# A hybrid encoder layer: the DVE steps of the triangular solve are given 36 units of other work in place of 24

## The chip, the core and the metric

The kernel runs on one core of one Trainium2 chip. The metric is the device time of one execution in microseconds; the time shown for a kernel is the median of its runs. The core has five engines with instruction queues of their own: TensorE (PE, with its weight loads shown apart as PEld), VectorE (DVE), ScalarE (ACT), GpSimd (POOL) and SyncE (SP, which issues most DMAs). Each works its queue off in order. An instruction that waits for another engine stops everything behind it in its own queue.

## The reference, cut to what matters

One layer over 2048 prompt rows and 8 x 16 sample rows of width 1024. Of the projected columns, 768 go to sliding-window attention and 1824 to an RWKV-7 mixer with 8 heads of 64; then come an output projection and a squared-ReLU feed-forward of width 4096:

```python
h = _rms(x, ln1_g)
p = h @ w_in
...
def step(S, inp):
    r_t, w_t, k_t, v_t, a_t, b_t = inp
    sa = jnp.einsum('bhij,bhj->bhi', S, a_t)
    S = S * w_t[:, :, None, :] + sa[..., None] * b_t[:, :, None, :] + v_t[..., None] * k_t[:, :, None, :]
    y = jnp.einsum('bhij,bhj->bhi', S, r_t)
    return S, y
...
x = x + jnp.concatenate([att, rw], axis=-1) @ w_out
u = jax.nn.relu(_rms(x, ln2_g) @ w_up)
x = x + (u * u) @ w_down
```

The kernel doesn't walk through the recurrence token by token. It takes chunks of 64 tokens, and within a chunk the coupling of the tokens is a unit lower triangular system of 64 x 64 per head. Its inverse is the "solve" of this document.

## The kernel before, in words

**Tiles and stages.** The rows are 17 tiles of 128: 0 to 15 are the prompt, 16 (`SMP`) the samples. The input projection (`in_proj`, matmuls at line 210) takes tiles 0 to 3 and 16, then 4 to 7, 8 to 11 and 12 to 15, in nine column pieces each. The feed-forward takes five groups of tiles: three tiles each in groups 0 to 3, and 12 to 16 in group 4. For each of 32 slices of the hidden width, `up` (line 1230) multiplies and squares; after every two of them `down` (line 1252) adds into `y`, by a DVE instruction for each bank (line 1254). All weights are used as a high and a low part. They are split at first use, by ACT (line 128) and POOL (line 132), and written back to DRAM for the next groups.

**Streams.** Attention, the mixer's preparation (`prep_stream`) and its chain over chunks (`chain_stream`) are Python generators. For each tile, in the order 0, 1, 2, 16, 3, 4, ... 15, `prep_stream` loads the projected rows, forms decays and keys, transposes them on PE (line 594), multiplies the coupling matrices (line 613) and calls `solve`; then the chain takes the tile. A generator yields a pair (units of other work wanted before it goes on, its own matrix work).

**The solve (line 648 on).** On DVE: four transposes bring the diagonal 16 x 16 blocks of `ma` into `WS` (line 653); six pairs of multiply (line 666) and reduce (line 668) invert the 8 x 8 blocks; lines 674 and 677 do that for the 16 x 16 blocks; lines 685, 686 and 689 write the inverses into `so` twice (once for the sample tile), for both orders of indices. Then, for prompt tiles only, PE takes over with four products of 16 matmuls of 64 x 64 (`product`, line 704), with a DVE or ACT step on all 128 columns after each (lines 709, 713, 717, 721), which fill the blocks off the diagonal. The first product reads `so` as the last line-689 transposes left it.

**What sets the order.** `Weaver` writes the instructions of the streams between those of the main work (`filler`: the projection or the feed-forward). Its clock is not time but units of matrix work: the filler and the streams add their own. A stream that yielded u units is due u times its pace later. The pace of prep and chain is 0.75, and 0.88 in the feed-forward. In the projection every due stream goes on after each piece of filler work. In the feed-forward there are slots:

```python
                if self.clock < self.slot:
                    continue
                for m in list(self.mains):
                    while self.step([m], 2.0):
                        pass
                self.slot = self.clock + 3.2
```

In a slot each stream goes on as long as it is due within 2.0 units. A group of the feed-forward waits until its tiles are in `done`. The last group's buffers take the place of the mixer's: once all tiles are done during group 3, its set-up (`stages`: loads, mixes, output projection at line 1188, norms with transposes at line 1143) is spread evenly over what is left of group 3's 32 steps. The other groups are set up in one block between two groups.

The launch uses a framework with a scheduler of its own (`schedule_with_timeline_sim=True`): the order written is a priority, and an instruction may be placed ahead of others that were written before it. The order that runs is the one after that.

Of the kernel before, what the change touches and what calls it, by code (L numbers as in the profile page):

```python
# [34 lines left out]
def hymba_kernel(  # L35
# [454 lines left out]
    def rw_prep(t, rp, loaded, so):  # L490
# [117 lines left out]
        for par in range(2):  # L608
# [12 lines left out]
            yield 4, 1  # L621
        pr = dict(t=t, art=art, m1=m1, lam=lam, ma=ma, so=so)
        yield from solve(ma, pr["so"], not smp, rp)

        yield "tail"
# [23 lines left out]
    def solve(ma, so, full, rp):  # L649
        EX, WS = rwc["EX"], rwc["WS"]  # L650
        for q in range(4):
            B, o = q // 2, 16 - 16 * (q % 2)
            ve.transpose(out=WS[32 * q:32 * q + 32, o:o + 512],  # L653
                         in_=ma[32 * B:32 * B + 32, :, 16 * q:16 * q + 16].rearrange("p s i -> p i s").unsqueeze(2)
                         .broadcast_to([32, 16, 2, 16]))
        Wv = WS[:, 16:528].rearrange("p (i j) -> p i j", i=16)
        blk = WS[:, 16:544].rearrange("p (b x) -> p b x", b=2)
        Db = blk[:, :, 0:256].rearrange("p b (i j) -> p b i j", i=8)
        ve.memset(blk[:, :, 0:256:33], 1.0)
        WT = rp.tile([P, 512], F32, name="tm", bufs=2)  # L660
        yield 4, 0
        for i in range(2, 8):
            if i in (5, 7):
                yield 4, 0
            tmp = WT[:, 0:2 * i * i].rearrange("p (b x y) -> p b x y", b=2, x=i)
            ve.tensor_tensor(out=tmp, in0=Db[:, :, i, 0:i].unsqueeze(2).broadcast_to([P, 2, i, i]),  # L666
                             in1=Db[:, :, 0:i, 0:i].rearrange("p b j a -> p b a j"), op=ALU.mult)
            ve.tensor_reduce(out=Db[:, :, i, 0:i], in_=tmp, axis=AX.X, op=ALU.add)

        tmp = WT[:, 0:512].rearrange("p (i a j) -> p i a j", i=8, a=8)  # L670
        zz = rp.tile([P, 64], F32, name="zz").rearrange("p (i a) -> p i a", i=8)
        L21 = Wv[:, 8:16, 0:8]
        for lh, rh, dst in ((L21, Db[:, 0, :, 0:8], zz), (Db[:, 1, :, 0:8], zz, L21)):
            ve.tensor_tensor(out=tmp, in0=lh.unsqueeze(2).broadcast_to([P, 8, 8, 8]),
                             in1=rh.rearrange("p j a -> p a j").unsqueeze(1).broadcast_to([P, 8, 8, 8]), op=ALU.mult)
            yield 2, 0
            ve.tensor_reduce(out=dst, in_=tmp, axis=AX.X, op=ALU.add)
        gp.memset(so[64:96, :, 32:64], 0.0)
        Ev = EX[:, 16:272].rearrange("p (i j) -> p i j", i=8)[:, :, 0:16]
        for w in range(2):  # L680
            if w == 1 and not full:
                break
            yield 2, 0
            src = Wv[:, :, 0:16] if w == 0 else Wv[:, :, 0:16].rearrange("p i j -> p j i")
            ve.tensor_scalar(out=Ev, in0=src[:, 0:8], scalar1=lanes[0], scalar2=None, op0=ALU.mult)
            ve.scalar_tensor_tensor(out=Ev, in0=src[:, 8:16], scalar=lanes[1], in1=Ev, op0=ALU.mult, op1=ALU.add)
            for q in range(4):
                r0, o = 32 * (q // 2) + 64 - 64 * w, 16 - 16 * (q % 2)
                ve.transpose(out=so[r0:r0 + 32, :, 16 * q:16 * q + 16].rearrange("p s (b i) -> p i b s", b=2),  # L689
                             in_=EX[32 * q:32 * q + 32, o:o + 256])  # L690
        if not full:
            return
        yield 4, 0
        lo, hi = slice(0, 64), slice(64, 128)
        G = rp.tile([P, 1024], F32, name="t4").rearrange("p (a h x) -> p a h x", a=2, h=8)
        Z = [rp.tile([P, 512], F32, name="tm", bufs=2).rearrange("p (h x) -> p h x", h=8) for _ in range(2)]
        sc = [so[:, 8 * c:8 * c + 8] for c in range(2)]

        def product(terms):

            ps = psR.tile([P, 8, 64], F32, name="sv")
            for h in range(8):
                for c, (lh, rh) in enumerate(terms):
                    pe.matmul(ps[64 * c:64 * c + 64, h], lh[:, h], rh[:, h], start=True, stop=True)  # L704
            return [ps[lo], ps[hi]]

        p = product([(ma[lo, 8 * c:8 * c + 8], sc[c][lo]) for c in range(2)])
        for c in range(2):
            ve.tensor_tensor(out=G[hi, c], in0=p[c], in1=offm.unsqueeze(1).broadcast_to([64, 8, 64]), op=ALU.mult)
        yield 4, 1  # L710
        p = product([(G[hi, c], sc[c][hi]) for c in range(2)])
        for c in range(2):
            ve.tensor_tensor(out=sc[c][hi], in0=p[c], in1=sc[c][hi], op=ALU.add)
        yield 4, 1
        p = product([(G[hi, c], sc[c][hi]) for c in range(2)])
        for c in range(2):
            ac.copy(out=Z[c][hi], in_=p[c])
        yield 4, 1
        p = product([(G[hi, c], Z[c][hi]) for c in range(2)])
        for c in range(2):  # L720
            ve.tensor_tensor(out=sc[c][hi], in0=p[c], in1=sc[c][hi], op=ALU.add)
        yield 3, 1
# [719 lines left out]
```

## Time and profile before

| | |
|---|---|
| time, median of 3 runs | 3015.76 us (3009.49 to 3020.29) |
| the profiled execution's own time | 3006.76 us |
| its span in the profile | 3005.0 us |
| granted PE clock, mean of the span | 0.976 of full speed |
| PE busy | 2860.8 us, 95% |
| DVE busy | 1816.4 us, 60% |
| ACT busy | 866.6 us, 29% |
| POOL busy | 663.4 us, 22% |

The span is the time from the first to the last instruction of one profiled execution. Busy times count an engine's instructions with their overlap taken out; matmuls are pipelined, so a busy PE need not be at its peak. In the trace the input projection ends at about 925 us, group 0 runs from about 960 to 1360 us, group 1 from 1420 to 1790, group 2 from 1830 to 2165, group 3 from 2224 to 2555 and group 4 from there to the end; the stretches between are set-up. A matmul in 32-bit words on 64 columns appears twice in the trace where the program has it once, so a product's 16 matmuls are 32 there.

### The profile page before, as it was taken

Reading aid. Unit: us, or ns where it says so; the run is one execution under the profiler, and the core shown is the slowest. Engines: PE = TensorE matmul, PEld = TensorE weight load, DVE = VectorE, ACT = ScalarE, POOL = GpSimd, SP = SyncE. Lnnn points to the kernel's source line nnn. Section 1 sums busy time; section 2 is a strip of 40 time slices with the busy share of each in tenths; the row PEclk is TensorE's granted clock in tenths of the full one; section 3 lists DMA queues with packets and bytes.
Section 4 is the critical chain, followed back from the end, with each engine's and each line's share of the span. In section 5 each row is a group of like instructions: output and inputs, shape, how many; then the busy total and the mean of one; then the engine's idle time right before and its main releaser. Section 6 shows DMA issues by size and latency. Waiting matters only on the chain.

```text
span 3005.0 us, 52176 instructions
## 1 busy us (share of the span) xinstructions
PE 2860.8 (95%) x20746; PEld 2540.4 (85%) x20746; DVE 1816.4 (60%) x3411; ACT 866.6 (29%) x2093; POOL 663.4 (22%) x625
## 2 busy tenths in 40 slices
PE   7989999989997988989999999999999999999999
PEld 7978878878877877878888888888889999989988
DVE  3557687673775688786677875786633344344344
ACT  5342443443343433432222223222221021111111
POOL 2122432432434766751101110111000000000000
PEclk9999999999998999999999999999999999999999
DMA  7866565554748777877666675665676566544444
GB/s 267 292 217 196 174 209 180 181 175 155 235 157 298 284 269 286 293 265 252 217 228 235 231 270 179 240 215 201 223 293 242 210 218 239 180 154 149 147 154 147
DMA packets 192141, 657.71 MB, mean 219 GB/s; under 512 B 31885, under 2 KB 88989, under 8 KB 145818
## 3 DMA queue, kind: packets, MB, share of 16 engines
q1 hardware_dynamic: 176346, 557.64, 54.9%
q0 software_dynamic: 15552, 96.74, 7.8%
q8 instruction: 164, 2.69, 0.4%
q14 instruction: 79, 0.65, 0.1%
HBM read 486.37 MB, written 154.73 MB: 213 GB/s over the span
## 4 chain that ended last, share of the span: by engine, by line
PE 70%; DVE 14%; DMA 8%; issue 3%; ACT 2%; POOL 2%; SPq 0%; DVEq 0%; ACTq 0%; POOLq 0%
PE ffn L1230 21%; PE ffn L1252 21%; PE acc L210 11%; PE ffn L1188 3%; DMA w<-wp 2%; PE sv L704 2%; PE op L1188 2%; DVE so L689 2%; DMA xs<-pa 1%; DVE WS L653 1%; DMA pc<-pb 1%; DVE y L1254 1%; POOL w L132 1%; PE rk L613 1%; DVE tm L666 1%
## 5 line engine op out<-in xcount | busy, mean ns | idle before, releaser
L1230 PE MATMUL ffn<-ghh,w 128*128 128x384 f32 (+1 forms) x3072 | 779.2, 331 | 0.1
L1252 PE MATMUL ffn<-w,sh 128*128 128x512 f32 x2176 | 694.7, 401 | 17.3 <-DVE y L1254 13.9
L1230 PEld LDWEIGHTS ffn<-ghh,w 128*128 128x128 f32 x3072 | 548.8, 190 | 8.3 <-issue 2.9
L1254 DVE SCALAR_TENSOR_TENSOR y<-ffn,rs,y 128x512 f32<-128x512 f32 x544 | 401.8, 748 | 203.3 <-PE ffn L1252 201.6
L1230 PE MATMUL ffn<-ghl,w 128*128 128x384 f32 (+1 forms) x1536 | 505.9, 329 | 0.0
L1252 PEld LDWEIGHTS ffn<-w,sh 128*128 128x128 f32 x2176 | 403.8, 190 | 109.0 <-DVE y L1254 16.3
L210 PE MATMUL acc<-w,hh 128*128 128x304 f32 (+1 forms) x2128 | 463.9, 309 | 22.2 <-ACT ev L215 9.2
L1252 PE MATMUL ffn<-w,sl 128*128 128x512 f32 x1088 | 427.6, 396 | 2.4 <-DVE sl L1237 2.2
L210 PEld LDWEIGHTS acc<-w,hh 128*128 128x128 f32 x2128 | 351.0, 194 | 44.0 <-DMA w<-wp 11.2
L1235 DVE TENSOR_TENSOR tq<-tq 128x384 f32<-128x384 f32 (+1 forms) x192 | 111.4, 580 | 391.9 <-ACT tq L1234 391.0
L210 PE MATMUL acc<-w,hl 128*128 128x304 f32 (+1 forms) x1064 | 319.7, 303 | 0.0
L1234 ACT ACTIVATE tq<-ffn 128x384 f32<-128x384 f32 (+1 forms) x192 | 91.0, 474 | 709.4 <-PE ffn L1230 689.7
L1230 PEld LDWEIGHTS ffn<-ghl,w 128*128 128x128 f32 x1536 | 290.9, 189 | 5.2 <-issue 1.9
L1252 PEld LDWEIGHTS ffn<-w,sl 128*128 128x128 f32 x1088 | 205.7, 189 | 50.5 <-DVE sl L1237 4.7
L132 POOL TENSOR_TENSOR w<-ws,w 128x512 fp32r<-128x512 f32 x144 | 196.1, 1380 | 109.7 <-ACT w L128 104.7
L210 PEld LDWEIGHTS acc<-w,hl 128*128 128x128 f32 x1064 | 206.3, 194 | 3.9 <-issue 3.4
L1236 ACT CAST sh<-tq 128x384 fp32r<-128x384 f32 (+1 forms) x192 | 95.2, 496 | 344.6 <-PE ffn L1252 220.4
L1188 PE MATMUL ffn<-w,ghh 128*128 128x256 f32 x768 | 146.2, 291 | 19.5 <-ACT w L128 10.3
L1237 DVE TENSOR_TENSOR sl<-tq,sh 128x384 fp32r<-128x384 f32 (+1 forms) x192 | 117.1, 610 | 62.4 <-ACT sh L1236 62.2
L1188 PEld LDWEIGHTS ffn<-w,ghh 128*128 128x128 f32 x768 | 122.8, 196 | 22.6 <-ACT w L128 10.5
L215 ACT ACTIVATE ev<-acc,xr_rs 128x304 f32<-128x304 f32 (+1 forms) x153 | 75.9, 501 | 151.1 <-PE acc L210 103.9
L1188 PE MATMUL ffn<-w,ghl 128*128 128x256 f32 x384 | 110.2, 288 | 0.0
(349 smaller groups left out, 4084.8 us busy)
## 6 DMA issues: line engine op xcount, KB each, us to landing
w<-wp SPq DMA_DIRECT2D x288, 1024.0 KB
wp<-w POOLq DMA_DIRECT2D x72, 1024.0 KB, 7.3
w<-wp SPq DMA_DIRECT2D x72, 608.0 KB
w<-wp SPq DMA_DIRECT2D x36, 512.0 KB
ws<-in_wup_dram SPq DMA_DIRECT2D x32, 512.0 KB
ws<-in_wdn_dram SPq DMA_DIRECT2D x32, 512.0 KB
pb<-eb SPq DMA_DIRECT2D x102, 152.0 KB
pa<-ev SPq DMA_DIRECT2D x102, 152.0 KB
```

The source lines that it names most:

```text
L132: gp.tensor_tensor(out=wl[:, c], in0=ws[:, c], in1=wh[:, c].bitcast(F32), op=ALU.subtract)
L210: pe.matmul(acc[:, 0:n], a[:, kk], b[:, c], start=(kk == 0 and m == 0), stop=(kk == 7 and m == 2))
L215: ac.activation(out=ev, in_=acc[:, 0:n], func=AF.Copy, scale=hT[t][2])
L689: ve.transpose(out=so[r0:r0 + 32, :, 16 * q:16 * q + 16].rearrange("p s (b i) -> p i b s", b=2), in_=EX[32 * q:32 * q + 32, o:o + 256])
L1188: pe.matmul(pss[j // 2][:, o:o + 256], a[:, kk, self.col(t)], w[:, c], start=(kk == 0 and m == 0 and j % 2 == 0), stop=(kk == 7 and m == 2 ...
L1230: pe.matmul(ps, w[:, wc], a[:, kk, c], start=(kk == 0 and m == 0), stop=(kk == 7 and m == 2))
L1234: ac.activation(out=tq, in_=ps, func=AF.Relu)
L1235: ve.tensor_tensor(out=tq, in0=tq, in1=tq, op=ALU.mult)
L1236: ac.copy(out=sh[:, c], in_=tq)
L1237: ve.tensor_tensor(out=sl[:, c], in0=tq, in1=sh[:, c].bitcast(F32), op=ALU.subtract)
L1252: pe.matmul(ps, a[:, tc_], w[:, fc], start=(f == 0 and m == 0), stop=(f == 1 and m == 2))
L1254: ve.scalar_tensor_tensor(out=yt[:, c], in0=ps, scalar=self.rs2[t], in1=yt[:, c], op0=ALU.mult, op1=ALU.add)
```

## The change

Five yields in `solve` are made half as long again: 4 to 6, and 2 to 3. Three of these lines are met twice (in the loops), so a prompt tile's solve yields 36 units in place of 24: before the first row, before rows 5 and 7, between multiply and reduce of lines 674 and 677 (twice), before each of the two writings of `so`, and before the first product. No instruction is added or taken away.

```diff
         WT = rp.tile([P, 512], F32, name="tm", bufs=2)
-        yield 4, 0
+        yield 6, 0
         for i in range(2, 8):
             if i in (5, 7):
-                yield 4, 0
+                yield 6, 0
...
         for lh, rh, dst in ((L21, Db[:, 0, :, 0:8], zz), (Db[:, 1, :, 0:8], zz, L21)):
...
-            yield 2, 0
+            yield 3, 0
             ve.tensor_reduce(out=dst, in_=tmp, axis=AX.X, op=ALU.add)
...
         for w in range(2):
             if w == 1 and not full:
                 break
-            yield 2, 0
+            yield 3, 0
...
         if not full:
             return
-        yield 4, 0
+        yield 6, 0
         lo, hi = slice(0, 64), slice(64, 128)
```

**Tile 5's first product on PE, in group 0.** The names are the bank written, then the two operands; `w2` is a weight, `sh` and `sl` the high and low parts of the hidden values, `ma` the coupling matrices, `so0` the inverse. Before:

```order
L1252 MATMUL ffn_12452<-w2_12444,sl_12160 128x512
L1252 MATMUL ffn_12452<-w2_12444,sh_12294 128x512 x2
L1252 MATMUL ffn_12452<-w2_12444,sl_12295 128x512
L704 MATMUL sv_12425<-so0_2757,ma_12130 64x64 x16
L1252 MATMUL ffn_12460<-w2_12444,sh_12159 128x512 x2
L1252 MATMUL ffn_12460<-w2_12444,sl_12160 128x512
```

The change, at the same place of the `down` step, and where the last of the product stands:

```order
L1252 MATMUL ffn_12848<-w2_12840,sl_12592 128x512
L1252 MATMUL ffn_12848<-w2_12840,sh_12726 128x512 x2
L1252 MATMUL ffn_12848<-w2_12840,sl_12727 128x512
L704 MATMUL sv_13001<-so0_2757,ma_12562 64x64 x10
L1252 MATMUL ffn_12856<-w2_12840,sh_12591 128x512 x2
L1252 MATMUL ffn_12856<-w2_12840,sl_12592 128x512
```

```order
L1252 MATMUL ffn_12982<-w2_12966,sl_12883 128x512
L1252 MATMUL ffn_12990<-w2_12966,sh_12882 128x512 x2
L1252 MATMUL ffn_12990<-w2_12966,sl_12883 128x512
L704 MATMUL sv_13001<-so0_2757,ma_12562 64x64 x3
L1252 MATMUL ffn_13028<-w2_13020,sh_12770 128x512 x2
```

Of the 16 matmuls that stood together, ten stand at the same place of a `down` step, and the other six follow in pieces of one, two and three.

**The norms' transposes of group 4 on PE, within group 3** (`op` are the banks of its set-up, `y` its rows). Before, a piece of them between the matmuls of a `down` step:

```order
L1252 MATMUL ffn<-w_25361,sh 128x512 x2
L1252 MATMUL ffn<-w_25361,sl 128x512
L1143 MATMUL op<-cst,y 128x128 x6
L1252 MATMUL ffn<-w_25361,sh 128x512 x2
L1252 MATMUL ffn<-w_25361,sl 128x512
```

The change, in the last `up` step of group 3 and, between its matmuls, the first of group 4 (320 columns):

```order
L1230 MATMUL ffn<-ghh,w_26020 128x384
L1143 MATMUL op<-cst,y 128x128 x16
L1230 MATMUL ffn<-ghh,w_26179 128x320
L1230 MATMUL ffn<-ghl,w_26179 128x320
L1230 MATMUL ffn<-ghh,w_26179 128x320 x2
L1230 MATMUL ffn<-ghl,w_26179 128x320
L1230 MATMUL ffn<-ghh,w_26179 128x320 x2
L1143 MATMUL op<-cst,y 128x128 x8
```

Before, the 40 transposes stand in pieces of 1 to 7 over several steps; in the change they stand close together, in pieces of 4 to 16, where group 4 begins.

## Rows read from the trace of the kernel before

**Rows 1.** The page's first part: busy us (share of the span) x instructions of each engine.

```profile
PE 2860.8 (95%) x20746; PEld 2540.4 (85%) x20746; DVE 1816.4 (60%) x3411; ACT 866.6 (29%) x2093; POOL 663.4 (22%) x625
```

**Rows 2.** Windows by stage: length, busy us (x) of each engine, clock, DMA.

```profile
core 0: us, PE busy (x) PEld busy (x) DVE busy (x) ACT busy (x) POOL busy (x), PEclk, DMA share, GB/s
...
960.00:1360.00 400.00, 366.95 (x2659) 312.69 (x2660) 307.23 (x484) 158.07 (x293) 254.02 (x223) 0.95 0.79 281
...
1420.00:1790.00 370.00, 368.40 (x2764) 316.70 (x2761) 263.26 (x484) 94.56 (x214) 50.91 (x39) 0.99 0.65 227
...
1830.00:2165.00 335.00, 331.61 (x2448) 286.37 (x2448) 227.14 (x415) 78.56 (x175) 37.33 (x28) 0.99 0.61 212
2165.00:2224.00 59.00, 51.58 (x419) 48.20 (x420) 30.34 (x74) 18.62 (x47) 2.94 (x2) 1.00 0.88 340
2224.00:2555.00 331.00, 331.00 (x1894) 307.92 (x1895) 127.58 (x236) 54.45 (x122) 0.00 (x0) 1.00 0.64 226
```

**Rows 3.** Waits of PE and its weight loads: us in total, times, longest us.

```profile
PEld sv L704 <- DVE so L689: 19.8, 9, 7.1
...
PE sv L704 <- DVE so L689: 16.6, 6, 6.7
PE ffn L1252 <- DVE y L1254: 13.9, 10, 6.8
```

**Rows 4.** Timeline, PE: first products of tiles 1, 5, 7, 15 [idle before <-releaser].

```profile
404.64 1.12 PE L704 MATMUL sv<-so,ma 64*64 64x64 f32 x16 [3.22 <-DVE so L689]
...
1092.35 1.97 PE L704 MATMUL sv<-so,ma 64*64 64x64 f32 x32 [4.93 <-DVE so L689]
...
1311.19 1.97 PE L704 MATMUL sv<-so,ma 64*64 64x64 f32 x32 [6.70 <-DVE so L689]
...
2112.46 0.74 PE L704 MATMUL sv<-so,ma 64*64 64x64 f32 x18 [0.40 <-DVE so L689]
```

**Rows 5.** Timeline, DVE: tile 5's solve (start us, us, instruction).

```profile
1059.10 3.19 DVE L653 STREAM_TRANSPOSE WS<-ma 32x512 f32<-32x512 f32 x3
...
1078.33 2.25 DVE L674 TENSOR_TENSOR tm<-WS,zz 128x512 f32<-128x512 f32 x1
...
1082.77 0.35 DVE L686 SCALAR_TENSOR_TENSOR EX<-WS,cst,EX 128x128 f32<-128x128 f32 x1
...
1086.93 2.85 DVE L686 SCALAR_TENSOR_TENSOR EX<-WS,cst,EX 128x128 f32<-128x128 f32 x1
1089.82 2.47 DVE L689 STREAM_TRANSPOSE so<-EX 32x256 f32<-32x256 f32 x4
```

**Rows 6.** Timeline, DVE: the same two lines at tile 13.

```profile
1909.39 1.18 DVE L674 TENSOR_TENSOR tm<-WS,zz 128x512 f32<-128x512 f32 x1
...
1916.88 0.44 DVE L686 SCALAR_TENSOR_TENSOR EX<-WS,cst,EX 128x128 f32<-128x128 f32 x1
```

**Rows 7.** Timeline, POOL, beside tile 5's solve.

```profile
1083.75 2.49 POOL L132 TENSOR_TENSOR w<-ws,w 128x512 fp32r<-128x512 f32 x2 [1.14 <-ACT w L128]
...
1087.13 2.49 POOL L132 TENSOR_TENSOR w<-ws,w 128x512 fp32r<-128x512 f32 x2
```

**Rows 8.** The chain of waits: start us, us, engine and line, matmuls.

```profile
2237.98 8.20 PE ffn L1252 x36
2246.19 8.34 PE ffn L1230 x48
```

**Rows 9.** Windows of 5 us after the waits of tiles 5 and 7.

```profile
1090.00:1095.00 5.00, 2.65 (x34) 2.44 (x35) 4.93 (x8) 0.00 (x0) 0.48 (x1) 0.53 1.01 391
1095.00:1100.00 5.00, 5.00 (x21) 4.25 (x20) 3.40 (x6) 1.56 (x2) 0.19 (x1) 0.79 0.33 139
...
1310.00:1315.00 5.00, 3.81 (x37) 3.30 (x38) 4.93 (x8) 0.00 (x0) 0.00 (x0) 0.50 0.95 379
```

**Rows 10.** Timeline, PE: tile 4's second and third products.

```profile
964.45 1.15 PE L704 MATMUL sv<-so,t 64*64 64x64 f32 x32 [0.99 <-DVE t L709]
...
967.51 1.76 PE L704 MATMUL sv<-so,t 64*64 64x64 f32 x28 [1.33 <-DVE so L713]
```

## The prediction

> **What bounds the kernel now.** I read the page's busy times first [rows 1], then the stages by windows [rows 2], the waits [rows 3], and last the timelines around single solves [rows 4 to 7]. TensorE (PE) is busy for 95% of the span and DVE for 60% [rows 1], so PE sets the time, and a change in DVE's work pays only where PE stands still for it. Idle PE, as window length less busy time, is 33.0 us in the first feed-forward group (960 to 1360 us), but only 1.6 us in the next and 3.4 us in the one after [rows 2]. The time left to win by better cover is therefore in the input projection and in group 0, and not in the middle of the feed-forward.
>
> The change aims at one wait: PE's first solve product (line 704) on the last DVE step of the tile's solve (line 689). It costs PE 16.6 us in six waits, the longest 6.7 us. The weight loader's view of it is 19.8 us; the two overlap, so I do not add them [rows 3]. Three of the six carry most of it: tile 1 with 3.22 us in the input projection, tile 5 with 4.93 us and tile 7 with 6.70 us in group 0 [rows 4]. Later tiles pay 0.40 us, such as tile 15 [rows 4]. Why group 0 pays more stands in DVE's rows. At tile 5 the step at line 686 took 0.35 us once and 2.85 us the other time, and the product at line 674 took 2.25 us [rows 5], where at tile 13 the same lines took 0.44 and 1.18 us [rows 6]. While the slow ones ran, POOL was splitting weights (line 132), 2.49 us for each pair [rows 7], which it does only where weights are used for the first time.
>
> **What the change does.** It removes and adds no instruction. It only makes the Weaver wait longer between the solve's parts, and its arithmetic decides how much. In the feed-forward the pace is 0.88, slots are at least 3.2 units apart, and a stream goes on in the same slot if it is due within 2.0 units. A yield of 2 is due after 1.76 and went on at once; a yield of 3 is due after 2.64 and waits for the next slot. A yield of 4 or 6 (3.52 or 5.28) mostly takes one slot in either case. So the four small yields become four slots. Working the Weaver's clock through, a tile's period in the feed-forward grows from 92 units to 108, and the last tile's chain ends at 2049 in place of 1809. The feed-forward needs each group's tiles later than that in both, so it never waits for a tile.
>
> But what runs is the scheduler's order, not the Weaver's. For tile 5 DVE has 46 rows from the first line-653 transpose to the last line-689 one, ten of them the feed-forward's own, before and now alike: DVE's part is not spread out at all. On PE the first product is no longer in one piece. Its first 10 matmuls stand where all 16 stood, and the last five come about 14 us of matrix work later, as the order rows of the change show. I work such cover out from the matmuls in the order, at 8.34/48 = 0.174 us for one of 384 columns and 8.20/36 = 0.228 us for one of 512 [rows 8]. From the tile's last line-613 product to the head of the first solve product, PE has 23.7 us of work for tile 5 before and now; for tile 15, 22.3 us in both. A head of a few matmuls stops PE's queue as well as a whole product does, so its wait stays. The other products do move, by 15 to 20 us for most tiles, but nothing waited long for those.
>
> **The sum,** against the profiled execution (3006.76 us, of which 3005.0 us are span; the median of the runs shown, 3015.76 us, is 9.0 us above it, and I carry the difference over to that):
>
> 1. Tile 7's wait. With the longer period its solve moves from group 0's steady part to the stage between groups 0 and 1, where POOL no longer splits weights. I take its 6.70 us [rows 4] as gone. The granted clock was 0.50 in the 5 us that followed [rows 9], the lower of the two levels: 3.81 us of busy PE at half speed is 1.9 us more. Together -8.6 us. Bounds: -8.6 (gone) and 0 (its head now has 15.5 us of cover in place of 23.9, and waits there as long).
> 2. Tile 5's wait. Head and DVE rows are unchanged: 0. Bounds: 0 and, if all goes, -4.93 us and the slow clock behind it, (1 - 0.53) x 2.65 + (1 - 0.79) x 5.00 = 2.3 us [rows 4, 9]: -7.2 us.
> 3. Tile 3, now solved as the input projection ends. Its four products stand within 4 us of matrix work; before, they took 18 us. Each needs the DVE or ACT step on the one before it. The nearest rows are tile 4's, which waited 0.99 and 1.33 us between its products [rows 10]. Three such gaps at 1.2 us, less the 2.3 us that tile 4 no longer pays: about +1 us; without any cover three gaps of 2 us, +4. As the whole solve also has less cover (14.1 us before its head, where no tile had under 18.6), I take +3. Bounds 0 and +7.
> 4. Group 4's set-up. It is spread over group 3's 32 steps now, since tile 15 is done when that group begins. In the change it starts at step 26 and all 40 transposes of the normalised rows stand at the group's end, as the second pair of order rows shows. Before, group 3 had no idle PE at all in 331 us, while the set-up of group 3 itself, which stands in one block, lost 59.00 - 51.58 = 7.4 us [rows 2]. The new one lies between the two: +3 us. Bounds 0 and +7.4.
> 5. Everything else is moved and not changed. About half a tile's work leaves the input projection and group 0 for group 3, where DVE is busy for 127.6 of 331 us [rows 2]. It is still PE work there: 0. Bounds -5 and +5, three of the smaller waits [rows 3, 10] either way.
>
> Sum: -8.6 + 0 + 3 + 3 + 0 = about -3 us. On the median's scale 3013 us.
>
> One rule bears on term 2. The row shows the line-686 step at 2.85 us beside POOL's 2.49 us pair [rows 5, 7], and I keep its whole wait because the order beside it has not changed. The Trainium skill, SBUF — State Buffer, section "Who interferes with whom", says that a DVE instruction with two SBUF inputs and a GpSimd instruction that reads SBUF exclude each other for a whole instruction, and that issue order decides who blocks. By that rule the delay hangs on which of the two starts first, and so may be gone at tile 5 though its rows stand where they stood: the two stretched steps lost 2.85 - 0.44 and 2.25 - 1.18 us, 3.5 us in all [rows 5, 6], and the sum would be -6 us in place of -3.
>
> **The rivals.** A, *the wait goes after all* (faster). If the heads find their data ready, tiles 1, 5 and 7 lose 3.2, 7.2 and 8.6 us, and the 2.3 us at tile 4 go too: -21 us, 2995 us. For it: later products really have 15 us more in front of them, and POOL need not meet tile 5 again. Against it: the heads have not moved.
>
> B, *heads pulled forward into group 0* (slower). In the change tiles 4, 5 and 6 are solved there, and tile 4's first two matmuls stand behind 19.2 us of matrix work, while DVE needs 33.2 us for such a solve (1059.10 to the 1092.29 at which the last transpose ends) [rows 5]. Cover of 23.7 and 23.9 us meant a wait before, and tile 6 with 26.1 us had none, so it decides below about 24 us. If tile 4 then pays what tile 7 paid (8.6 us) and tile 7's own four early matmuls keep theirs, term 1 becomes +8.6, and with terms 3 and 4 the sum is +14.6 us: 3030 us. Against it: tile 4 had only 18.9 us before and no wait, because PE stood still for weights there.
>
> C, *it does not do what it says*: the heads keep every wait, tile 7's too, and the moves cancel: 3016 us, within my middle case.
>
> **How the numbers follow.** A difference of 0.3%, 9 us, is about what a measurement of this kernel can tell from none. The forecast with C around it, within 9 us of 3015.76, gets 0.50; A gets 0.29, since it needs only two of its three waits; B 0.21, since it needs a new wait at tile 4 or idle PE in both terms 3 and 4 at their upper ends. The range reaches from A's 2995 with 2 us below it to B's 3030: 2993 to 3030 us.
>
> **What would show it.** In the profile of the changed kernel: the wait of line 704 on line 689 should still be there, at about 16.6 - 6.7 = 10 us, tile 5's at 4 to 6 us and tile 7's under 1 us (term 1 is wrong if it is over 3). The waits between tile 3's products should sum to 3 to 6 us. Idle PE in the last 60 us of group 3 should be 1 to 6 us. Line 704 should run until late in group 3 in place of ending at its beginning, and the middle of the feed-forward (groups 1 and 2) should stay under 5 us of idle PE each. I am wrong if the line-704 wait falls under 5 us (then A, and the heads did not matter), if tile 4 waits over 4 us (then B), or if the input projection as a whole moves by more than 8 us, of which nothing here tells.

## The result and the profile after

The changed kernel takes **3062.89 us** (median; 3059.67 to 3066.61), the kernel before in the same runs 3013.75 us (3007.24 to 3020.29). The ratio is 1.0156, 95% interval 1.0141 to 1.0172: slower by 1.56%, 47 us. The prediction was 3013 us, range 2993 to 3030, with 0.21 on slower. It was wrong, in sign and in size.

The page's busy line of the change, which answers to [rows 1]:

```profile
PE 2885.9 (94%) x20746; PEld 2549.9 (83%) x20746; DVE 1809.9 (59%) x3411; ACT 862.7 (28%) x2093; POOL 659.0 (22%) x625
```

The span is 3064.8 us, 59.8 more than before. PE has the same 20746 matmuls, 25.1 us more busy time, and so 34.7 us more idle time. The two profiled executions lie further apart than the medians: 3006.76 us is near the lower end of the kernel before, and 3066.61 is the highest of the change's six. The granted clock differs too: 0.965 to 0.969 in the change's six executions (mean 0.968), 0.969 to 0.976 (mean 0.973) in 13 executions of the kernel before. If all of PE's busy time goes with it, that is 2885.9 x (1 - 0.968/0.973), about 15 of the 47 us; this is an estimate. To see where the idle time is, I cut both traces at the same events: the last projection matmul (line 210), the first `up` (line 1230) of group 0, the first output projection (line 1188) of group 1's set-up and of group 3's, and the first `up` of group 4. Before (windows; columns as in [rows 2]):

```profile
0.00:875.00 875.00, 807.70 (x6660) 723.54 (x6661) 549.89 (x1149) 348.02 (x981) 265.92 (x288) 0.97 0.62 205
875.00:970.00 95.00, 74.71 (x647) 65.85 (x646) 61.09 (x130) 38.23 (x86) 49.55 (x44) 0.84 0.71 255
970.00:1357.00 387.00, 356.27 (x2516) 303.28 (x2515) 295.80 (x454) 148.08 (x266) 246.76 (x216) 0.95 0.78 280
1357.00:2175.00 818.00, 803.88 (x6228) 696.94 (x6227) 578.06 (x1104) 206.74 (x479) 98.27 (x75) 0.99 0.64 225
2175.00:2544.00 369.00, 361.61 (x2171) 338.20 (x2170) 144.46 (x283) 67.05 (x154) 2.94 (x2) 1.00 0.68 243
```

The change, the same stages:

```profile
0.00:875.00 875.00, 799.36 (x6460) 717.18 (x6460) 535.44 (x1115) 339.75 (x962) 262.60 (x287) 0.96 0.62 205
875.00:998.00 123.00, 84.87 (x758) 73.91 (x753) 69.09 (x144) 44.53 (x103) 50.58 (x45) 0.78 0.57 201
998.00:1358.00 360.00, 337.66 (x2272) 288.80 (x2272) 260.07 (x384) 134.52 (x231) 230.90 (x206) 0.96 0.81 294
1358.00:2167.00 809.00, 781.25 (x5663) 676.33 (x5659) 527.11 (x1005) 186.60 (x430) 87.39 (x67) 0.98 0.64 226
2167.00:2599.00 432.00, 422.37 (x3062) 378.77 (x3061) 224.03 (x441) 91.68 (x212) 27.51 (x20) 0.98 0.61 217
```

These rows show work that was moved and not paid back. The set-up and steps of group 3 have 891 matmuls more (3062 against 2171) and are 63 us longer. The stages from which they came have 898 fewer: 200 in the projection, 244 in group 0, 565 in groups 1 and 2 with the set-ups before them, less 111 more in group 0's set-up. They should have become shorter by as much. But the projection, with 200 matmuls fewer, still takes 875 us, and the set-up of group 0 is 28 us longer; group 0 and the middle stage give back 27 and 9 us. The loss is made early, although the end shows it.

Length less busy time is PE's idle time. By stage, worked out from such windows, cut at the same events (the table's runs are explained below; a label's first part, such as e3, stands for the run):

| idle PE, us | projection | set-up 0 | group 0 | to group 3's set-up | group 3 with set-up | group 4 | sum | busy |
|---|---|---|---|---|---|---|---|---|
| before | 67.3 | 20.3 | 30.7 | 14.1 | 7.4 | 4.4 | 144.2 | 2860.8 |
| the change | 75.6 | 38.1 | 22.3 | 27.8 | 9.6 | 5.4 | 178.9 | 2885.9 |
| e3, projection only | 76.4 | 34.2 | 29.6 | 29.0 | 7.9 | 4.4 | 181.3 | 2873.3 |
| e4, feed-forward only | 66.5 | 19.1 | 20.0 | 19.1 | 11.1 | 4.3 | 140.1 | 2881.3 |
| e9, change without four tiles | 70.6 | 27.0 | 19.8 | 16.3 | 8.9 | 4.8 | 147.4 | 2880.4 |
| e5, tile 3 and all behind late | 66.6 | 20.7 | 34.1 | 27.1 | 9.5 | 4.3 | 162.4 | 2879.0 |
| s4, only those behind tile 3 late | 70.5 | 26.9 | 21.0 | 24.2 | 6.3 | 4.6 | 153.5 | 2862.8 |
| s3_pace | 74.5 | 21.5 | 34.6 | 13.5 | 6.4 | 4.4 | 154.7 | 2875.9 |
| e1, only the 4s longer | 79.5 | 17.8 | 29.6 | 26.1 | 6.2 | 4.4 | 163.6 | 2886.1 |
| e2, only the 2s longer | 79.5 | 20.1 | 11.9 | 22.3 | 8.2 | 4.7 | 146.7 | 2899.1 |
| p6_16, as fast as before | 64.9 | 18.7 | 35.0 | 23.2 | 4.3 | 4.3 | 150.5 | 2863.5 |

Each row is one execution. The last row tells how much a column moves without a loss: p6_16 is as fast as the kernel before, and its stage up to group 3's set-up has 23.2 us of idle PE against 14.1. So the 27.8 us of the change there are not shown to be a loss, but its 38.1 us in group 0's set-up stand well clear of the 18.7 to 26.9 of runs without a loss.

The waits of PE in the change, which answer to [rows 3] (us in total, times, longest):

```profile
PE sv L704 <- DVE so L689: 18.3, 8, 6.5
PE ffn L1143 <- DVE ghl L143: 16.6, 3, 8.1
PE ffn L1252 <- DVE y L1254: 14.2, 10, 6.9
PE ffn L1188 <- DVE y L1193: 13.7, 3, 9.9
PE acc L210 <- DMA w<-wp: 12.6, 13, 3.4
...
PE acc L210 <- DVE hl L86: 5.8, 4, 3.5
```

The wait that the change aims at is not smaller: 18.3 us against 16.6 [rows 3]. Four others grew. In the kernel before, the wait of line 1143 on line 143 was 6.2 us, that of line 1188 on line 1193 4.7, line 210 on its weights 8.5, and line 210 on line 86 2.1 us. The first and the third grow without a loss too (19.4 us for line 1143 in p6_16, 12.6 for the weights in s4_delay4); only the other two stand out. The largest single ones, on PE's timeline of the change:

```profile
647.23 0.55 PE L210 MATMUL acc<-w,hh 128*128 128x304 f32 x2 [3.53 <-DVE hl L86]
...
882.64 1.98 PE L704 MATMUL sv<-so,ma 64*64 64x64 f32 x32 [5.32 <-DVE so L689]
886.20 1.98 PE L704 MATMUL sv<-so,t 64*64 64x64 f32 x32 [1.58 <-DVE t L709]
...
970.97 0.80 PE L1188 MATMUL ffn<-w,ghh 128*128 128x256 f32 x2 [9.93 <-DVE y L1193]
...
997.28 1.11 PE L1143 MATMUL ffn<-cst,y 128*128 128x128 f32 x4 [8.14 <-DVE ghl L143]
...
1175.12 1.12 PE L704 MATMUL sv<-so,ma 64*64 64x64 f32 x16 [6.47 <-DVE so L689]
```

The first is in the projection, the next four in group 0's set-up. At 882.64 it is tile 3's solve, which now stands behind the last projection matmul (874.6 us); before, its first product ran at 836.1 us, with 40 us of projection left. The rows at 647.23, 970.97 and 997.28 are waits of the main work on DVE, which was held by the mixer's rows; the last row is tile 5's first product, in group 0. DVE, ahead of the waits at 647.23 and 970.97:

```profile
643.16 1.04 DVE L653 STREAM_TRANSPOSE WS<-ma 32x512 f32<-32x512 f32 x1
...
646.49 0.68 DVE L86 TENSOR_TENSOR hl<-acc,hh 128x512 fp32r<-128x512 f32 x1
...
965.50 0.63 DVE L498 TENSOR_TENSOR xs<-xs,pc 128x456 f32<-128x456 f32 x1 [6.70 <-DMA pc<-pb]
969.95 0.63 DVE L498 TENSOR_TENSOR xs<-xs,pc 128x456 f32<-128x456 f32 x1 [3.81 <-DMA pc<-pb]
970.50 0.75 DVE L1193 TENSOR_TENSOR y<-ffn,y 128x256 f32<-128x256 f32 x2
```

The sample tile's solve starts at 639.96 us (before, at 611.61), and the row at 643.16 is the last of its four transposes; the split of the next tile's normalised rows (line 86), for which the projection waits, comes behind them. At 965 DVE stands for the DMA of tile 4's rows (line 498), and behind that instruction, in DVE's queue, wait the additions of group 0's output projection (line 1193). Ahead of 997.28 DVE had tile 4's solve between the line-143 rows.

### The profile page after: what moved, and what is told of

Same layout as the page of the kernel before. It is cut to its first block, busy times and chain, and to the rows that moved or that the text cites. A ratio compares the mean times of both kernels' runs of the same rounds, so it can differ in the third digit from the quotient of the medians.

```text
span 3064.8 us, 52188 instructions
## 1 busy us (share of the span) xinstructions
PE 2885.9 (94%) x20746; PEld 2549.9 (83%) x20746; DVE 1809.9 (59%) x3411; ACT 862.7 (28%) x2093; POOL 659.0 (22%) x625
## 5 line engine op out<-in xcount | busy, mean ns | idle before, releaser
L210 PE MATMUL acc<-w,hh 128*128 128x304 f32 (+1 forms) x2128 | 466.8, 311 | 29.3 <-DMA w<-wp 12.6
L564 POOL TENSOR_TENSOR s<-s,mhalf 128x8 f32<-128x8 f32 x17 | 31.5, 1853 | 436.8 <-DVE s L563 435.4
L215 ACT ACTIVATE ev<-acc,xr_rs 128x304 f32<-128x304 f32 (+1 forms) x153 | 75.6, 500 | 161.4 <-PE acc L210 122.4
```

The lines of the kernel that those rows point to most:

```text
L210: pe.matmul(acc[:, 0:n], a[:, kk], b[:, c], start=(kk == 0 and m == 0), stop=(kk == 7 and m == 2))
L215: ac.activation(out=ev, in_=acc[:, 0:n], func=AF.Copy, scale=hT[t][2])
L564: gp.tensor_tensor(out=s8, in0=s8, in1=mhalf[:, 0:8], op=ALU.pow)
```

## The experiments

All ratios are to the kernel before, run beside them, with 95% intervals. Clock units are the Weaver's, worked out by running its arithmetic without the chip. Letters in the expectations: S, the four tiles solved in the projection get longer, tile 3 falls behind the projection's end, and it costs there; L, the longer period and the late end in group 3 cost; W, the two waits of 9.93 and 8.14 us in group 0's set-up are the loss; P, any shift of phase costs; the other letters are told where they stand.

### Which yields: by size

e1_fours keeps the 2s and makes only the 4s a 6; e2_twos keeps the 4s and makes only the 2s a 3.

```diff
-        yield 4, 0
+        yield 6, 0
```

> Only the yields of 4 become 6; those of 2 stay. In the feed-forward a tile keeps a period of about 92 units of the Weaver's clock, and the last chain ends as group 3 begins (1835 against 1809 before). Theory L (the time is lost because four more slots a tile let the mixer end late, in group 3): 3014 us, within 9 of before, with no line-704 work after group 3's first steps. Theory S (it is lost at the start, because tiles 3 and 4 now fall into the tail of the projection and the set-up of group 0): 3035 to 3050, since tile 3 is late here too. Theory P (every order has its own collisions on DVE, and the length of the period decides nothing): anywhere from 3005 to 3065, with the waits at places of its own.

> Only the yields of 2 become 3, which are the four more slots: the period is 108 units and the last chain ends at 2028, late in group 3, as in the change. Theory L: 3063 us, within 9 of the change. Theory S: 3035 to 3050. Theory P: anywhere from 3005 to 3065.

Measured: e1_fours 3051.7 us, 1.0109 (1.0084 to 1.0135); e2_twos 3046.04 us, 1.0089 (1.0068 to 1.0109). Either half costs more than half of what both cost. Which yield is longer matters little; the parts don't add up to the change (1.98% against 1.56%). Theory L falls with both, and S names about the right times (3035 to 3050). But S puts the price behind the projection's end, and in these two runs group 0's set-up has no more idle PE than before (17.8 and 20.1 us, table). Tile 3's first product runs at 880.6 us in both, ahead of the last projection matmul at 885.4 and 889.1 us. The projection ends at 886 and 890 us, with 79.5 us of idle PE and some 150 matmuls fewer than before, where it ended at 875.

### Which yields: by place

The Weaver's slot is None in the projection and a number in the feed-forward. e3_proj has the longer yields only in the projection (tiles 0, 1, 2, the samples, and tile 3's first part), e4_ffn only behind it.

```diff
-        yield 4, 0
+        yield (6 if wv.slot is None else 4), 0
```

> The longer yields hold only until the feed-forward begins, the old ones after that: the order of the projection and the set-up of group 0 begins as in the change, the period is 92 and the last chain ends at 1843. Theory L: 3014 us, within 9. Theory S: about 3040, as 12 us more of waits in the projection and 25 us in the set-up of group 0 come with it, less 10 us in group 0. Theory P: anywhere from 3005 to 3065.

> The old yields until the feed-forward begins, the longer ones after that: the projection is that of before, the period is 108 and the last chain ends at 2020, late in group 3. Theory L: 3055 to 3063 us. Theory S: 3014 to 3025. Theory P: anywhere from 3005 to 3065.

Measured: e3_proj 3056.81 us, **1.0126** (1.0098 to 1.0154); e4_ffn 3025.84 us, **1.0028** (1.0015 to 1.0041). The two do add up, to 1.0154. L falls again; S is close to both, though both are slower than it said (about 3040, and 3014 to 3025). Some four fifths of the loss come from the longer yields that are met in the projection, for which I had no price but term 3's. In e4_ffn the change does what it is meant to do. Its waits of PE:

```profile
PE sv L704 <- DVE so L689: 7.8, 5, 2.6
```

That is 8.8 us less than before (2.0 of them in the projection, where nothing was changed), and PE's idle time falls to 140.1 us. It is still not faster, since busy time grows by 20.5 us (table). The clock explains part of it between these two executions (mean 0.972 against 0.976), but not the 0.28%: over all executions it is 0.972 against 0.973. What grows are the groups of lines 704 and 1252: together by 13.5 us here, by 17.1 in the change, and by 18.3 in e9_all4 (below), whose clock is the 0.976 of before. All runs with the longer yields in the feed-forward have 11.8 us or more; all others have 9.3 or less, e3_proj 4.1, p6_16 none. Two of these groups, before and in e9_all4 (busy us, mean ns of one, idle before them):

```profile
L1252 PE MATMUL ffn<-w,sh 128*128 128x512 f32 x2176 | 694.7, 401 | 17.3 <-DVE y L1254 13.9 <-ACT sh L1236 3.4
L704 PE MATMUL sv<-so,ma 64*64 64x64 f32 x512 | 24.5, 241 | 16.7 <-DVE so L689 16.6
```

```profile
L1252 PE MATMUL ffn<-w,sh 128*128 128x512 f32 x2176 | 704.6, 404 | 24.4 <-DVE y L1254 11.9 <-ACT sh L1236 7.5 <-DMA w<-wp 1.9
L704 PE MATMUL sv<-so,ma 64*64 64x64 f32 x512 | 30.4, 239 | 6.2 <-DVE so L689 6.1
```

These are the products in pieces and the 512-column matmuls between which they now stand. That the pieces are the reason is likely, but no run changes them alone. The weight loader's gaps before line 704 grow with them, from 19.0 us in 72 before to 29.1 in 99 in e4_ffn:

```profile
PEld sv L704 <- issue: 29.1, 99, 1.5
```

e9_all4 is the counter-test: the change, but tiles 0, 1, 2 and the samples keep the old yields.

```diff
-        yield from solve(ma, pr["so"], not smp, rp)
+        yield from solve(ma, pr["so"], not smp, rp, t in (0, 1, 2, SMP))
...
-        yield 6, 0
+        yield (4 if old else 6), 0
```

> The change, but the solves of tiles 0, 1, 2 and 16 keep the old yields; tile 3 and all later tiles have the longer ones. Tile 3's preparation then ends at 676 units, just before the projection ends at 679, while the feed-forward is written with the period of 108. Theory S (the larger part of the loss is that tile 3 falls behind the projection's end): 3022 to 3032 us, as the run with the longer yields in the feed-forward alone. Rival (the longer yields cost wherever they stand, in proportion to the tiles that have them): 3050 us or more.

Measured: 3025.86 us, **1.0022** (1.0004 to 1.0039). That is as S said. Four tiles' yields carry 1.34 of the 1.56%; with them goes tile 3's lateness, which they cause. The long period of 108 units and the late end in group 3, which e9_all4 keeps, are worth 0.2 to 0.3%.

### What in them: that tile 3 is late, or that later tiles are

In the change tile 3's solve ends at 699.8 units, 26 behind the projection's end (673.9); before, at 667.7, 15 ahead of it (682.7). e5_delay3 is the kernel before with a wait of 32 units ahead of tile 3's load, and s3_half with half of it. From tile 3 on, e5_delay3's steps have the same clocks as e3_proj's. s4_delay4 has the 32 units ahead of tile 4 in place of tile 3.

```diff
+            if t == 3:
+                yield 43, 0
             loaded = rw_load(t)
```

> The kernel before, its solve untouched (24 units everywhere), but tile 3's rows are loaded 32 units of the Weaver's clock later, so that from the end of the projection on everything is written as in the run with the longer yields in the projection alone. Theory S (the lateness of tile 3 alone is the price, whatever caused it): 3040 to 3057 us, with the first line-1230 matmul 20 to 28 us later than before. Theory D (the price lies in how the longer yields change the solves of tiles 0, 1, 2 and 16 in the projection): 3010 to 3025.

> The kernel before with half of that delay in front of tile 3 (16 units): its solve ends at 683 units, 6 units behind the projection's end at 677, and not 22 to 26 behind it. If what counts is the matrix work that is left beside tile 3 the cost lies between, 3020 to 3030 us; if it is only the side of the end on which tile 3 stands, 3034 us as with the whole delay; if the place costs nothing below some size, 3016 us.

> The kernel before, in which tile 4 and all behind it start 32 units later, while tile 3 keeps its place (the run with the delay in front of tile 3 put tile 4 and all behind it at the same units, and cost 0.66%, 20 us). Theory T, in which tile 3 itself is what costs: 3010 to 3024 us. Rival (the shift of all later tiles costs, by where their solves fall in the groups): 3030 us or more, with 15 us or more of new stalls between group 0's end and group 2's.

Measured: e5_delay3 3036.18 us, **1.0066** (1.0043 to 1.0089); s3_half 3026.01 us, 1.0028 (1.0012 to 1.0043); s4_delay4 3019.08 us, **1.0006** (0.999 to 1.0021). e5_delay3 lies between its two theories (S from 3040, D to 3025 us); s3_half and s4_delay4 are as the slope and theory T had them. With all later tiles late, and at nearly the same clocks, the place of tile 3 makes 0.6%, 18 us. On the chip its first product then ran at 867.3 us, the end of the projection, in place of 840.6 (s4_delay4). It looks like a slope and not a step: half the delay costs about half, with the product at 845.6, still 18 us ahead of the last projection matmul. So tile 3 need not fall over the projection's end to cost something.

The same shift further back, 8, 16 and 24 units behind tile 6's load (p6_8, p6_16, p6_24), asked whether any change of phase costs, because the kernel before happens to stand well:

```diff
-            yield 6, 0
+            yield 22 if t == 6 else 6, 0
```

> The kernel before with one delay in the middle of group 0: 8 units more after the load of tile 6, nothing else. Every later tile is about 7 units late against the feed-forward's steps; the period of 92 stays. Theory P (the place at which a solve meets the steps and the set-ups decides, whatever the length of the yields): the time moves by more than 9 us, to between 3020 and 3045, with other waits in groups 1 and 2. Rival (such a shift is harmless as long as the mixer ends in time): 3014 us, within 9.

> As the run with 8 units, with 16: all tiles after 6 are some 14 units late. Theory P: between 3005 and 3045, and not in line with the runs at 8 and 24 units. Rival: 3014 us, within 9.

> As the run with 8 units, with 24: all tiles after 6 are 17 to 21 units late, close to where the run with only the yields of 4 made longer has them. Theory P: between 3005 and 3045, not in line with the runs at 8 and 16 units, and in groups 1 to 3 with the 10 to 15 us of new waits that that run has there. Rival: 3014 us, within 9.

Measured: 3015.86, 3019.72 and 3015.87 us; 0.9991 (0.9976 to 1.0006), 0.9996 (0.9981 to 1.0011), 1.0001 (0.9983 to 1.0018). Theory P falls for shifts of up to 24 units behind tile 6; shifts elsewhere can cost, as e8_ffnshort below.

### The rest: the longer yields ahead of tile 3

Between e5_delay3 (+0.66%) and e3_proj (+1.26%) the solves of the four tiles ahead of tile 3 differ, and the part of tile 3's that falls into the projection. The table puts the difference at the projection (66.6 to 76.4 us of idle PE) and at group 0's set-up (20.7 to 34.2). s3_pace is e3_proj with a shorter pace for tile 3's preparation, so that everything from its end on has the clocks of the kernel before.

```diff
+            prep[3] = (0.88 if wv.slot is not None else 0.38 if t == 3 else 0.75)
             loaded = rw_load(t)
```

> The longer yields in the input projection alone (3056.8 us before this edit, +39 us), and tile 3's preparation goes on at pace 0.38 in place of 0.75, so that it ends at 667.0 units, before the projection's end at 682.7; from there on every step of the weaver stands at the clock that it has in the kernel before. Theory T (the loss hangs on tile 3's place, behind the projection's end, and on what that shifts): 3013 to 3025 us, with the stretch from the projection's last matmul to the first `up` near the 94.6 us of before. Rival Q (it is lost at the four tiles that are solved in the projection with the longer yields): 3040 us or more, with the projection's stalls 12 us above those of before as in the change.

Measured: 3029.3 us, **1.0036** (1.002 to 1.0051), between the two expectations: 0.9% of e3_proj's 1.26% comes back, and 0.36%, 11 us, stays. The projection's idle time stays with it (74.5 us, 7 more than before), as the rival had it. But the run is not as clean as meant: tile 3 ended early by the Weaver's clock and not on the chip. Its first product on PE:

```profile
883.81 1.34 PE L704 MATMUL sv<-so,ma 64*64 64x64 f32 x32 [4.05 <-DVE so L689]
```

So it still ran behind the projection. What came back lies in group 0's set-up (34.2 to 21.5 us of idle PE, as little as before) and in the stage behind group 0 (29.0 to 13.5), where the tiles behind tile 3 now stood as before. Their shift alone had cost nothing (s4_delay4). So four long solves and a late tile 3 together cost 11 us when the tiles behind stand as before, and the effects don't add up: tiles behind tile 3 that are late cost some 27 us when tile 3 runs behind the projection and the four solves are long (e3_proj against s3_pace), and 2 us when neither is so. Why is open.

### Attempts on single waits, and on other places

e6_hold4 is the change with tile 4's load held back until the first `up` (tile 4's rows and solve were what DVE had in front of the waits of 9.93 and 8.14 us).

```diff
+            if t == 4:
+                yield lambda: bool(begun)
```

> The change, but tile 4's rows are loaded only when the first step of group 0 begins, so that neither its additions (line 498), which waited for DMAs in front of PE's output projection, nor its solve stand in group 0's set-up. Theory W (those two waits of PE, 9.9 and 8.1 us, are the price of the set-up): 3043 to 3048 us. Rival (the work comes back later: each tile is done 34 units later still): 3063 us, within 9 of the change, or more.

Measured: 3053.08 us, 1.0097 (1.007 to 1.0124), 18 us of the 47 back, between the two expectations. In its profile the set-up has 33.9 us of idle PE, 4 less than the change; group 0 (18.4) and the stage behind it (21.4) have 10 less together, and group 3 with its set-up 4 more (13.8). Theory W is half right at most: the largest single waits there are now 5.7, 5.0 and 4.8 us, and others have taken most of the place of the two.

h1_proj_hold, h2_before_hold and h3_change_hold deal out nothing of a chain or preparation between the projection's end and the first `up` (e3_proj, the kernel before and the change, in this order).

```diff
+                if hold[0] and m in (chain, prep):
+                    continue
```

> The longer yields in the input projection alone (3056.8 us before this edit, +39), and the weaver deals out nothing of a chain or of a preparation between the projection's end and the first `up` of group 0: tile 3's overdue work stands in group 0's steps. Theory U (the loss is tile 3's work standing where there is little matrix work beside it, in group 0's set-up): the first `up` comes 20 to 30 us earlier than in the same kernel without the edit (there about 998), the set-up falls from 120.6 to some 100 us, and the time is about 3030 us or less. Theory V (the loss is carried on: what does not wait there waits in group 0's steps, or the projection itself has already lost it): 3057 us +-9, the first `up` earlier and the steps of group 0 longer by as much.

> The kernel before, with its yields, and nothing of a chain or of a preparation dealt out between the projection's end and the first `up`. Theory U: the kernel before has only the rest of tile 3's work there, 3005 to 3014 us. Theory V: 3014 to 3030 us, later tiles stand a little later and nothing is won.

> The change itself (36 units everywhere), and nothing of a chain or of a preparation dealt out between the projection's end and the first `up`. Theory U: the first `up` 20 us or more earlier than the change's 998.5 us, and the time 3040 us or less. Theory V: 3063 us +-9, with the first `up` earlier and the steps of group 0 or the stages behind it longer by as much.

Measured: 3038.38 us, 1.0061 (1.0042 to 1.0081); 3030.91 us, 1.0044 (1.0027 to 1.006); 3059.39 us, 1.0141 (1.0116 to 1.0166). They don't tell the theories apart, since they did not do what they say: tile 3's products still ran at 882.4 us in h1_proj_hold and 881.7 in h3_change_hold, and the set-up kept its idle time (34.5 and 30.3 us). The Weaver had dealt that work out later, so the framework's scheduler must have moved it forward. Holding costs the kernel before 13 us and gives e3_proj 20 back.

e7_early (half the yields in the projection) and e8_ffnshort (4s to 2s in the feed-forward alone) go the other way from the kernel before.

```diff
-        yield 4, 0
+        yield (2 if wv.slot is None else 4), 0
```

> The kernel before with shorter yields in the solve (12 units in place of 24) until the feed-forward begins, the old ones after: tiles 3 and 4 are both prepared before the projection ends. Theory S: the earlier the better, 2995 to 3010 us, with the first line-1230 matmul earlier than before by up to 10 us. Rival (what is packed into the projection costs there what it saves behind it, as solve products wait longer for DVE): 3014 us, within 9, or up to 3030.

> The kernel before with shorter yields in the feed-forward alone (4 becomes 2): a period of about 75 units in place of 92, the last chain ends at 1615 in place of 1809. Theory L in its weak form (a shorter period saves as the longer one cost 9 us with the projection left alone): 3005 to 3010 us. Rival (with less matrix work before them the products wait for DVE): 3025 to 3050, with the line-704 wait on line 689 over 30 us.

Measured: 3023.53 us, 1.0025 (1.0004 to 1.0047), and 3047.06 us, 1.0077 (1.0048 to 1.0105). Both are as their rivals said in time, and the theories that foresaw a gain fall. But e8_ffnshort was slow for another reason than the rival's: the wait that was to exceed 30 us is 8.3 us. Earlier than before wins nothing either. No version beat the kernel before.

## Why the prediction was wrong

**Term 1 (tile 7's wait, -8.6 us)** was right as a mechanism. At 1424.39 us the first matmuls of tile 7's product run with no wait in front of them:

```profile
1423.78 0.69 PE L1230 MATMUL ffn<-ghh,w 128*128 128x384 f32 x3
1424.39 0.45 PE L704 MATMUL sv<-so,ma 64*64 64x64 f32 x8
```

But the line-704 wait as a whole did not fall to my 10 us. It is 18.3: tile 3's new wait of 5.3 us, tile 5's 6.5, and 6.5 in six smaller ones.

**Term 2 (tile 5's wait stays, 0)** was right, if a little small: 6.47 us, against 4.93 [rows 4] and my 4 to 6. DVE's rows at tile 5 and POOL's beside them:

```profile
1161.14 2.20 DVE L674 TENSOR_TENSOR tm<-WS,zz 128x512 f32<-128x512 f32 x1
...
1165.52 0.35 DVE L686 SCALAR_TENSOR_TENSOR EX<-WS,cst,EX 128x128 f32<-128x128 f32 x1
...
1169.70 2.85 DVE L686 SCALAR_TENSOR_TENSOR EX<-WS,cst,EX 128x128 f32<-128x128 f32 x1
```

```profile
1160.77 3.70 POOL L132 TENSOR_TENSOR w<-ws,w 128x512 fp32r<-128x512 f32 x2
...
1169.90 2.49 POOL L132 TENSOR_TENSOR w<-ws,w 128x512 fp32r<-128x512 f32 x2
```

The same two steps are stretched as before, line 686 to the same 2.85 us [rows 5], though everything around them has shifted by 80 us. The -6 us that I worked out from the lock rule of the Trainium skill (SBUF — State Buffer, "Who interferes with whom": issue order decides who blocks) did not come. The rows agree that the two engines exclude each other: POOL's pair took 3.70 us beside DVE's 2.20, and the line-686 step ended 0.16 us after POOL's pair. Who issued first they don't tell: at line 686 DVE's row starts 0.20 us ahead of POOL's, and yet DVE is the one that was held.

**Term 3 (tile 3 at the projection's end, +3, bounds 0 and +7)** is the first that failed, by its size. The wait between its products, which I had put at 3 to 6 us, is 1.58 us, and the one ahead of the first is 5.32: 6.9 together, within the bounds. But I priced the place by tile 3's own waits, and left out who queues behind its rows and tile 4's on DVE in the set-up. There the idle time of PE rose from 20.3 to 38.1 us, with the main work's waits of 9.93 and 8.14 us the largest, and the clock was 0.78 where it had been 0.84. These waits do not come from tile 3's place alone: in e5_delay3 and s3_pace, where its first product also runs at or behind the projection's end, the set-up has 20.7 and 21.5 us. Tile 3's lateness measured 0.6% with the tiles behind it late as well (e5_delay3 less s4_delay4), 18 us in place of 3; with those at their old place it and the four long solves together cost 11 us (s3_pace).

**Term 4 (group 4's set-up, +3)** was right: the last 60 us of group 3 have 1.0 us of idle PE, at the low end of the 1 to 6 expected.

```profile
2540.00:2600.00 60.00, 58.97 (x438) 56.79 (x436) 17.70 (x49) 11.44 (x30) 0.00 (x0) 1.00 0.49 173
```

**Term 5, "everything else is moved and not changed … 0", bounds -5 and +5,** is the step that failed most. It was a guess by number of instructions, and the bounds of ±5 us were taken from small waits, with no stage looked at. In its place the runs show 1.26%, 38 us, for the longer yields in the projection alone (e3_proj), with term 3's tile 3 among them, and 0.28%, some 8 us, for those behind it (e4_ffn). The half tile of work that leaves the early stages doesn't shorten them: the projection lost 200 matmuls and 8.3 us of busy time, and took on 8.3 us of idle time. In all profiles with the four long solves it has 72 to 76 us of idle PE, with half of the lengthening (e1_fours, e2_twos) 79.5, with the old yields 65 to 71. One of the new meetings is the sample tile's solve with line 86 (3.53 us at 647.23); it is not the whole reason, since e1_fours has 2.1 us of waits on line 86, as before, and the 79.5 us all the same. Nor did "still PE work there: 0" hold for busy time, which grew by 25.1 us. Idle time alone does not even give every loss: e2_twos lost 0.89% with 2.5 us more idle PE and 38.3 us more busy time than before. Which waits make the loss, beyond the place where it arises, stays open. The prediction said itself what would break it, an input projection that moves, "of which nothing here tells". That sentence was a term without a price, and the range should have held it. The projection's end did not move at all, but only because work had left it. None of my three signs of being wrong appeared: I had no sign for a set-up.

The middle of the feed-forward I had expected under 5 us of idle PE for each group. It is 4.1 us in group 1 and 5.6 in group 2; the other 18 of the stage's 27.8 us lie in the two set-ups and at their edges (before, some 9), of which I had said nothing:

```profile
1419.00:1765.00 346.00, 341.94 (x2411) 293.28 (x2411) 223.19 (x406) 81.44 (x184) 37.94 (x29) 0.99 0.62 216
1821.00:2167.00 346.00, 340.40 (x2333) 291.12 (x2329) 234.65 (x429) 78.56 (x177) 39.26 (x30) 0.98 0.64 223
```

**The rivals.** A needed the waits at the heads to go; in e4_ffn, with the projection left alone, half of that time does go (16.6 to 7.8 us), and more busy time of PE takes it back. B's wait at tile 4 is not there: its product started 8 us after its data. B's sign was right, by luck and by none of its mechanism. C is out.

## What to carry to other kernels

Where streams are woven by yields, a longer yield moves everything behind it on every stage, not only the step that it stands in. Before pricing the step, find the stage whose cover ends (here the projection) and ask which piece of work comes close to that edge. Look there at the waits of the main work that queues behind the moved work, and not only at the moved work's own. Here no sum of single waits gave the loss. So try the edit in one stage at a time: limited to the feed-forward this one cost 0.3%, in the projection alone 1.3%.

## What the runs showed that I had not expected

Moving the same 32 units of delay by one tile, from tile 4 to tile 3, takes the cost from 0.06% to 0.66%, and half of it at tile 3 costs 0.28% with the tile still inside the projection. And a stream's clock does not set its place on the chip: in s3_pace tile 3 was due 33 units earlier than in e3_proj (667 in place of 700), and its first product ran 2 us earlier (883.8 against 885.7 us). Last, PE's busy time is no measure of its work: the same 20746 matmuls took 2860.8 us before, 2880.4 in e9_all4 at the same mean clock of 0.976, and 2899.1 us in e2_twos.
